# A hybrid decoder layer on one core: the merge of the attention groups' outputs is put behind the sample's third group and the fourth head pair

## The chip, the core and the metric

The kernel runs on one core of a Trainium2 chip. The core has a TensorE (PE) for matrix products, a VectorE (DVE), a ScalarE (ACT) and a GpSimd (POOL) for element-wise work, and queues of DMA transfers that these engines or SyncE (SP) issue. Each engine runs its own instructions in the order in which the program emitted them, and waits for the others at semaphores. The metric is the device time of one execution in microseconds (us).

## The reference, cut to what matters

One inference step of one layer: a prompt of 512 tokens and 8 sample tokens (each with a cache of 4096 positions) pass the same weights. On the same normalised input run an attention in three groups (windows 128, 512 and 2048 with dilations 1, 4 and 16; 8 heads of 64 each) and an RWKV-7 recurrence with 16 heads. The three groups' outputs are merged by their log-sum-exp, each branch is projected and multiplied by a sigmoid gate, and an output projection and a SwiGLU follow.

```python
A_GROUPS = ((128, 1), (512, 4), (2048, 16))
...
    s = jnp.einsum('bgnqhd,bgnkhd->bgnhqk', qb.astype(jnp.float32), kb.astype(jnp.float32)) * HEAD_DIM ** -0.5
    p, lse = masked_softmax(s, valid[:, None])
    o = jnp.einsum('bgnhqk,bgnkhd->bgnqhd', p, vb.astype(jnp.float32))
...
    def step(S, inp):
        r_t, w_t, k_t, v_t, kk_t, a_t = inp
        sa = jnp.einsum('bhij,bhj->bhi', S, -kk_t)
        S = (S * w_t[:, :, None, :] + sa[..., None] * (kk_t * a_t)[:, :, None, :]
             + v_t[..., None] * k_t[:, :, None, :])
        return S, jnp.einsum('bhij,bhj->bhi', S, r_t)
```

## The kernel before

All products are of fp32 values that are split in a high and a low part, so that one k-tile of a projection is three matmuls (`hh,whi`, `hl,whi`, `hh,wlo`) of 128 x 260, 260 being half of the 520 tokens. Weights come as `raw` by DMA; ACT makes `whi` of them and DVE `wlo`. Every instruction goes through one helper, so each row of the profile names its line, 380; rows are told apart by their tiles.

The program is written as many small generators, one for each piece of work: the projections, the attention heads of a group, `sample_group(g)` for the sample tokens of group g, the eight head pairs of the recurrence (in steps `pair`, `chain`, group norm, output `OB`), the sixteen gate jobs (products for the sigmoid gates), the projection of the attention branch (pa), of the recurrent branch (pb), and so on. A planner runs them one step at a time at build time. It keeps a model of each engine's clock, plays the recurrence's jobs first where they are ready, and uses pa and the gate jobs as filler for PE. Waits between generators (`wv.until("merge")`, and `wv.take`/`wv.give` for locks) hold only at build time: they decide the order of emission, and the hardware's waits are the data's own.

What the change touches:

- `sample_group(g)` (line 891 on) scans the cache of group g for the eight sample tokens. For the third group (g = 2) these are eight K tiles and eight V tiles `kt` of 128 x 512, each loaded by a DMA that POOL issues, and for each a product and a reduction on DVE. They use two buffers, `kt`. Line 895 lets the third group wait for "merge", as long as `MERGE_AT` is negative.
- `merge()` (line 1489 on) computes the three groups' factors and stores them as `FD` in DRAM. Behind that, for each of four head pairs and three groups, POOL issues loads of a group's output `oo` (from `OTD`) and of its factors `fb` (from `FD`, broadcast to 64 partitions each, two transfers), into the same two buffers `kt`. DVE multiplies, in twelve operations on `oac` and eight on `oo`, and the sum goes to `OAD`.
- Lines 1518 to 1520, between the store of `FD` and the head pairs, make the merge wait for "sample" 2 and "pair" `MERGE_AT` if `MERGE_AT` is not negative.
- The lock "kt" is held by the merge from its first head pair to its last, and the lock "gq" (one buffer, `oac`, also used by the group norm) for each head pair.
- The split of the merged output for the attention branch's projection, `oa_load` (line 1646), waits for "merge" and for the last head pair.

In the old order the merge begins when the third group's heads are done (`rw_open`, line 1099, spawns it), and the sample's third group stands behind it.

Of the kernel before, what the change touches and what calls it, by code (L numbers as in the profile page):

```python
# [36 lines left out]
SHIFT0 = 4608  # L37
GATE0 = 7968
RESERVE = 0
MERGE_AT = -1  # L40
SAMPLE_AT = -1
PLAIN = 4
EARLY = 4
# [422 lines left out]
def program(tc, I, O):  # L466
# [425 lines left out]
    def sample_group(g):  # L892
        if g:
            yield from wv.until("sample", g - 1)
        if g == 2 and MERGE_AT < 0:
            yield from wv.until("merge")
# [592 lines left out]
    def merge():  # L1489
# [27 lines left out]
        G.dma_start(out=FD[:].rearrange("r h g l -> (r h) g l"), in_=ms[:, :, 0])  # L1517
        if MERGE_AT >= 0:
            yield from wv.until("sample", 2)
            yield from wv.until("pair", MERGE_AT)  # L1520
        yield from wv.take("kt")
# [612 lines left out]
```

## Time and profile before

| | |
|---|---|
| median of 3 runs | 1293.06 us |
| lowest and highest run | 1292.16 and 1295.9 us |
| profiled execution, its own time | 1299.81 us |
| its span on the core | 1298.0 us |
| mean granted TensorE clock | 0.985 of full speed |

The page of the profile gives busy times by engine and by line; answers of the trace give the same by stretches of time, by tile, and in order of time. Times in them are from the start of the span. A row in order of time has the start, the duration, the engine, the operation, the tiles (written <- read), the shapes and, in brackets, how long the engine was idle before it and what released it. Buffer numbers are left out there. The prompt's attention fills the span up to about 360 us; the recurrence runs from there to about 825 us; the output projection and the SwiGLU follow.

### The profile page before, as it was taken

How to read it: one execution, taken by the hardware profiler on the slowest of the kernel's cores; microseconds unless marked ns; L12 is line 12 of the kernel's file. 1: busy time of each engine (PE TensorE's matmuls, PEld its weight loads, DVE VectorE, ACT ScalarE, POOL GpSimd, SP SyncE). 2: the span in 40 equal slices, each digit the busy share in tenths (PEclk: the TensorE clock that was granted, in tenths of full speed). 3: DMA queues.
4: the chain of work that ended last, by engine and by line, in shares of the span. 5: the costliest groups of instructions: out<-in, count | busy, mean ns of one | idle time of the engine just before them, and what ended most of it. 6: DMA issues, size and time to landing. Idle time of an engine off the chain costs nothing.

```text
span 1298.0 us, 29596 instructions
## 1 busy us (share of the span) xinstructions
PE 1246.1 (96%) x11594; PEld 1178.2 (91%) x11594; DVE 933.4 (72%) x2448; ACT 648.2 (50%) x1638; POOL 176.0 (14%) x273
## 2 busy tenths in 40 slices
PE   7999999999989989999999999999999999999996
PEld 6998999989978888888888888999999999999996
DVE  6956866954769998879886765565798888873333
ACT  5244244266666655576775585323444444442220
POOL 1300100100123332122123112121000000010000
PEclk9999999999999999999998999999999999999998
DMA  6532654644245545553346355465233323343331
GB/s 218 157 95 91 209 178 146 208 137 160 73 121 152 145 143 149 153 156 104 89 126 184 101 168 169 139 218 191 92 99 98 98 98 98 98 143 90 90 103 66
DMA packets 93420, 173.76 MB, mean 134 GB/s; under 512 B 42672, under 2 KB 47824, under 8 KB 93280
## 3 DMA queue, kind: packets, MB, share of 16 engines
q1 hardware_dynamic: 60880, 102.46, 25.8%
q0 software_dynamic: 15792, 50.73, 12.9%
q10 hardware_dynamic: 16608, 18.68, 4.3%
q8 instruction: 91, 1.49, 0.5%
q14 instruction: 49, 0.40, 0.1%
HBM read 135.33 MB, written 30.07 MB: 127 GB/s over the span
## 4 chain that ended last, share of the span: by engine, by line
PE 59%; DVE 18%; issue 11%; DMA 6%; ACT 4%; POOL 2%; SPq 0%; ACTq 0%; DVEq 0%; POOLq 0%
PE mm L380 39%; PE ax L380 15%; PE ch L380 5%; DVE wlo L380 3%; DMA fb<-FD 1%; DVE X L380 1%; DVE xt L380 1%; DMA kt<-vcache 1%; DVE qk L380 1%; DVE raw L380 1%; DMA sw<-raw 1%; DVE sw L380 1%; DVE k L380 1%; DVE GH L380 1%; DVE oac L380 1%
## 5 line engine op out<-in xcount | busy, mean ns | idle before, releaser
L380 PE MATMUL mm<-hh,whi 128*128 128x260 f32 x1136 | 340.3, 300 | 0.8 <-ACT gt L380 0.8
L380 PE MATMUL mm<-hh,wlo 128*128 128x260 f32 x1136 | 326.0, 287 | 7.4 <-DVE wlo L380 7.0
L380 PE MATMUL mm<-hl,whi 128*128 128x260 f32 x1136 | 326.0, 287 | 0.0
L380 ACT CAST whi<-raw 128x1024 fp32r<-128x1024 f32 (+2 forms) x213 | 184.2, 866 | 255.8 <-PE mm L380 185.0
L380 DVE TENSOR_TENSOR wlo<-raw,whi 128x1024 fp32r<-128x1024 f32 (+2 forms) x213 | 211.5, 993 | 86.4 <-ACT whi L380 81.7
L380 PEld LDWEIGHTS mm<-hh,whi 128*128 128x128 f32 x1136 | 215.9, 190 | 13.3 <-issue 5.8
L380 PEld LDWEIGHTS mm<-hh,wlo 128*128 128x128 f32 x1136 | 216.0, 190 | 10.0 <-DVE wlo L380 9.2
L380 PEld LDWEIGHTS mm<-hl,whi 128*128 128x128 f32 x1136 | 215.9, 190 | 1.3
L380 PE MATMUL mm<-fh,whi 128*128 128x260 f32 x308 | 87.2, 283 | 0.3 <-DVE g L380 0.3
L380 PE MATMUL mm<-fh,wlo 128*128 128x260 f32 x308 | 87.1, 283 | 0.0
L380 PE MATMUL mm<-fl,whi 128*128 128x260 f32 x308 | 87.1, 283 | 0.0
L380 PE MATMUL mm<-h2l,whi 128*128 128x260 f32 x264 | 74.8, 283 | 0.0
L380 PE MATMUL mm<-h2h,wlo 128*128 128x260 f32 x264 | 74.6, 282 | 0.0
L380 PE MATMUL mm<-h2h,whi 128*128 128x260 f32 x264 | 74.6, 282 | 0.0
L380 PE MATMUL ax<-h2h,wlo 128*128 128x260 f32 x264 | 74.5, 282 | 0.0
L380 PE MATMUL ax<-h2l,whi 128*128 128x260 f32 x264 | 74.5, 282 | 0.0
L380 PE MATMUL ax<-h2h,whi 128*128 128x260 f32 x264 | 74.3, 281 | 0.0
L380 DVE TENSOR_TENSOR xt<-X,LT 128x60 f32<-128x60 f32 (+24 forms) x248 | 59.7, 241 | 3.6
L380 DVE TENSOR_TENSOR X<-X,xt 128x60 f32<-128x60 f32 (+24 forms) x248 | 56.1, 226 | 3.8
L380 PEld LDWEIGHTS mm<-fh,whi 128*128 128x128 f32 x308 | 58.1, 188 | 0.8 <-issue 0.4
L380 PEld LDWEIGHTS mm<-fh,wlo 128*128 128x128 f32 x308 | 57.9, 188 | 0.0
L380 PEld LDWEIGHTS mm<-fl,whi 128*128 128x128 f32 x308 | 57.9, 188 | 0.0
(427 smaller groups left out, 3122.0 us busy)
## 6 DMA issues: line engine op xcount, KB each, us to landing
raw<-w_in SPq DMA_DIRECT2D x77, 512.0 KB, 4.0
raw<-w_gate SPq DMA_DIRECT2D x22, 512.0 KB, 3.8
raw<-w_up SPq DMA_DIRECT2D x22, 512.0 KB, 3.8
raw<-w_down SPq DMA_DIRECT2D x16, 512.0 KB, 3.5
kt<-kcache POOLq DMA_DIRECT2D x24, 256.0 KB, 3.7
kt<-vcache POOLq DMA_DIRECT2D x24, 256.0 KB, 3.6
sw<-raw ACTq DMA_DIRECT2D x64, 65.0 KB, 3.7
GD<-gt ACTq DMA_DIRECT2D x16, 260.0 KB, 3.0
```

Of the source, the lines that this page charges most:

```text
L380: r = f(*a, **k)
```

## The change

One constant is changed.

```diff
 SHIFT0 = 4608
 GATE0 = 7968
 RESERVE = 0
-MERGE_AT = -1
+MERGE_AT = 3
 SAMPLE_AT = -1
 PLAIN = 4
 EARLY = 4
```

It acts at two places of the code:

```python
        if g == 2 and MERGE_AT < 0:
            yield from wv.until("merge")
...
        if MERGE_AT >= 0:
            yield from wv.until("sample", 2)
            yield from wv.until("pair", MERGE_AT)
        yield from wv.take("kt")
```

So the sample's third group no longer waits for the merge, and the head pairs of the merge wait for that group and for the head pair with index 3, the fourth, of the recurrence. As the planner's clocks and the locks see other work, the order changes from the end of the attention to the beginning of the output projection. The numbers of instructions on each engine stay as they were.

In the rows below, tiles carry the numbers that the program gives them. On DVE, before, at the first head pair of the recurrence (`k` and `sg` are its features, `tw` its scan; `oac` and `oo` are the merge's):

```order
L380 TENSOR_TENSOR wlo_4576<-raw_4457,whi_4575 128x1024
L380 COPY bvs<-tmp_4292 128x8
L380 SCALAR_TENSOR_TENSOR k_4518<-pb_4517,mu,k_4518 128x511
L380 SCALAR_TENSOR_TENSOR k_4518<-shift,mu,k_4518 128x8
L380 TENSOR_SCALAR sg_4743<-k_4518,feat 128x8
L380 TENSOR_TENSOR oac_4633<-oo_4374,fb_4376 128x4x128
L380 SCALAR_TENSOR_TENSOR tw_4630<-smask,tw_4630 128x512
L380 TENSOR_TENSOR oo_4641<-oo_4641,fb_4643 128x512
L380 TENSOR_TENSOR oac_4633<-oac_4633,oo_4641 128x4x128
```

And on DVE now, at the end of the attention heads (`PT` are the last heads' probabilities), where the sample's third group begins (`kt` times `sv`, reduced to `sc`):

```order
L380 COPY PT_4065<-ax_4126 128x512
L380 COPY PT_4065<-ax_4138 128x512
L380 TENSOR_TENSOR kt_4145<-kt_4145,sv_4102 128x512
L380 TENSOR_TENSOR kt_4147<-kt_4147,sv_4102 128x512
L380 TENSOR_REDUCE sc_4144<-kt_4145 128x8
L380 TENSOR_REDUCE sc_4144<-kt_4147 128x8
L380 TENSOR_TENSOR wlo_4250<-raw_4047,whi_4249 128x1024
L380 SCALAR_TENSOR_TENSOR k_4203<-pb_4202,mu,k_4203 128x511
L380 SCALAR_TENSOR_TENSOR k_4203<-shift,mu,k_4203 128x8
L380 TENSOR_TENSOR st_4722<-sv_4102 128x64
L380 TENSOR_SCALAR sg_4314<-k_4203,feat 128x8
```

The first row of the merge now stands about 180 rows of DVE further down, and the cache tiles stand where the merge stood and ahead of it.

On POOL, before, around the store of `FD` (`GH`, `AR` and `st` belong to the recurrence):

```order
L380 DMA FD<-ms 96x1x128
L380 TENSOR_TENSOR GH_4411<-GH_4411,DN_4277 64x8x64
L380 DMA fb_4376<-FD 64x4x128 x2
L380 DMA oo_4641<-OTD 128x512
L380 DMA fb_4643<-FD 64x4x128 x2
L380 DMA oo_4921<-OTD 128x512
L380 DMA fb_4923<-FD 64x4x128 x2
L380 TENSOR_TENSOR st_4603<-st_4603,sg_4290 128x512
```

And on POOL now, around the same store:

```order
L380 DMA kt_4433<-kcache 128x512
L380 DMA kt_4521<-kcache 128x512
L380 TENSOR_TENSOR GH_4450<-GH_4450,DN_4301 64x8x64
L380 DMA FD<-ms 96x1x128
L380 TENSOR_TENSOR AR_4318<-AR_4318,PC_4311 128x448
L380 DMA kt_4589<-kcache 128x512
L380 TENSOR_TENSOR GH_4451<-GH_4451,DN_4301 64x8x64
L380 DMA kt_4731<-vcache 128x512
```

The loads of `fb` stood directly behind the store that they read; now the loads of the cache stand there, and the first load of `fb` comes 18 rows after the store.

On PE, before, at the transposes (`ax<-ident,KB`) of the last head pair's group norm: `hh`, `hl` rows are a gate job's, and `OB` rows the recurrent branch's projection.

```order
L380 MATMUL mm_11568<-hh,wlo_11409 128x260
L380 MATMUL mm_11568<-hh,whi_11408 128x260
L380 MATMUL mm_11568<-hl,whi_11408 128x260
L380 MATMUL ax_11591<-ident,KB_9764 128x128 x4
L380 MATMUL mm_11568<-hh,wlo_11409 128x260
L380 MATMUL mm_11626<-OB_11290,whi_11545 128x260 x2
L380 MATMUL mm_11626<-OB_11290,wlo_11546 128x260
L380 MATMUL mm_11626<-OB_11350,whi_11545 128x260 x2
```

And on PE now, at the same transposes (`OB_11607` is the output of head pair 6, `OB_11721` that of head pair 7, the last):

```order
L380 MATMUL mm_11643<-OB_11607,whi_11399 128x260
L380 MATMUL mm_11643<-OB_11607,wlo_11400 128x260
L380 MATMUL ch_11669<-OB_11607,whi_11603 128x260
L380 MATMUL ch_11669<-OB_11607,wlo_11604 128x260
L380 MATMUL ch_11700<-OB_11607,whi_11603 128x260
L380 MATMUL ch_11700<-OB_11607,wlo_11604 128x260
L380 MATMUL ax_11691<-ident,KB_10009 128x128 x4
L380 MATMUL mm_11590<-OB_11721,whi_11399 128x260
L380 MATMUL mm_11643<-OB_11721,whi_11399 128x260
L380 MATMUL ch_11669<-OB_11721,whi_11603 128x260
```

The gate jobs' rows that stood ahead of the transposes are now further up, all sixteen jobs before the last head pair's chain; behind the transposes the rows that read the last pair's output stand first.

## The prediction

> **What bounds the kernel now.** I read the page's totals first, then busy time by stretches, then the waits and the timeline of the stretches that lose TensorE time.
>
> ```profile
> span 1298.0 us, 29596 instructions
> PE 1246.1 (96%) x11594; PEld 1178.2 (91%) x11594; DVE 933.4 (72%) x2448; ACT 648.2 (50%) x1638; POOL 176.0 (14%) x273
> ```
>
> TensorE (PE) is busy for 96% of the span, so a re-ordering that removes no matmul can only win what PE loses in gaps or at a low clock. Where it loses is read from the stretches; the columns are the stretch, its length, then busy time (and instructions) of PE, weight loads, VectorE (DVE), ScalarE (ACT) and GpSimd (POOL), then the granted clock, the DMA share and GB/s.
>
> ```profile
> 320.00:340.00 20.00, 19.98 (x192) 18.52 (x192) 9.79 (x45) 13.49 (x39) 2.23 (x4) 1.00 0.28 96
> 340.00:360.00 20.00, 20.00 (x169) 19.36 (x168) 18.90 (x40) 10.57 (x26) 3.98 (x4) 1.00 0.22 65
> 360.00:400.00 40.00, 32.84 (x291) 30.66 (x290) 29.01 (x72) 22.11 (x55) 13.80 (x18) 0.96 0.48 134
> 400.00:520.00 120.00, 111.30 (x1134) 100.95 (x1133) 110.39 (x366) 74.71 (x188) 34.44 (x50) 0.99 0.53 143
> 520.00:580.00 60.00, 59.29 (x766) 51.88 (x766) 50.16 (x152) 38.61 (x135) 14.15 (x22) 1.00 0.59 165
> 580.00:600.00 20.00, 16.62 (x184) 14.79 (x183) 17.36 (x57) 15.38 (x46) 3.37 (x3) 0.91 0.26 85
> 600.00:680.00 80.00, 78.90 (x862) 70.40 (x860) 69.85 (x270) 59.64 (x194) 16.24 (x22) 1.00 0.36 108
> 680.00:700.00 20.00, 17.28 (x157) 15.56 (x157) 16.27 (x47) 8.82 (x19) 6.09 (x9) 0.83 0.56 163
> 700.00:800.00 100.00, 99.47 (x1311) 85.90 (x1310) 63.02 (x233) 69.96 (x245) 21.29 (x37) 0.98 0.49 149
> 800.00:822.00 22.00, 19.66 (x194) 18.38 (x193) 13.70 (x40) 8.36 (x18) 3.23 (x6) 0.92 0.46 156
> 822.00:840.00 18.00, 17.35 (x140) 16.73 (x140) 8.95 (x13) 6.00 (x11) 2.15 (x4) 1.00 0.45 138
> 802.50:806.00 3.50, 1.72 (x16) 1.45 (x15) 2.19 (x8) 2.63 (x6) 0.54 (x1) 1.00 0.13 46
> 806.00:809.40 3.40, 3.40 (x29) 3.17 (x28) 3.16 (x11) 0.35 (x1) 0.55 (x1) 0.50 0.67 222
> ```
>
> From 360 to 822 us PE stands idle for about 26 us: 7.2 in 360 to 400, 8.7 in 400 to 520, 3.4 in 580 to 600, 2.7 in 680 to 700, 2.3 in 800 to 822, and little elsewhere. In 400 to 520 the reason is plain: DVE is busy for 110.4 of 120 us, so **DVE is the bound there**, with the merge and the sample's cache scan both in that stretch. The last two rows show a second price: a 3.5 us stretch with PE half idle is followed by one of 3.4 us at half clock, which costs 1.7 us more.
>
> **The change part by part.** No instruction is removed or added; PE's matmuls and DVE's work are the same in number. The merge and the sample's third group exchange places, and the planner, which fills PE's time with whatever is ready, then places the sixteen gate jobs and the output projection otherwise. Four terms follow.
>
> (a) *From 340 to about 540 us.* In the old order the merge starts as soon as the last attention heads are done, and its first steps wait for loads that could not start earlier.
>
> ```profile
> DVE oac L380 <- DMA fb<-FD: 7.2, 2, 6.4
> DVE oo L380 <- DMA fb<-FD: 6.1, 3, 4.1
> ```
>
> ```profile
> 361.99 0.23 DVE L380 TENSOR_SCALAR sg<-k,feat 128x8 f32<-128x8 f32 x1
> 368.63 1.10 DVE L380 TENSOR_TENSOR oac<-oo,fb 128x512 f32<-128x512 f32 x1 [6.41 <-DMA fb<-FD]
> 369.65 1.20 DVE L380 TENSOR_TENSOR_SCAN tw<-smask,tw 128x512 f32<-128x512 f32 x1
> 374.91 0.69 DVE L380 TENSOR_TENSOR oo<-oo,fb 128x512 f32<-128x512 f32 x1 [4.05 <-DMA fb<-FD]
> ```
>
> The waits rows read: in total, times, longest. DVE's queue is in order, so the scan at 369.65, which the recurrence needs, stands 6.4 us behind the broadcast factors fb. These waits sum to 7.2 + 6.1 = 13.3 us, and they go, because FD is written long before the merge now reads it. In their place DVE gets the cache tiles, whose loads can stand ahead of it too:
>
> ```profile
> L380 DVE TENSOR_TENSOR kt<-kt,sv x24: 672/688/712, 112.2 to 548.8; 128x512 f32<-128x512 f32 x24
> L380 DVE TENSOR_REDUCE sc<-kt x24: 667/679/705, 113.4 to 550.8; 128x8 f32<-128x512 f32 x24
> ...
>   DMA kt<-kcache: 7.2, 7
>   DMA kt<-vcache: 6.8, 5
> ```
>
> ```profile
> L380 DVE TENSOR_TENSOR oac<-oac,oo x8: 1079/1100/1132, 375.6 to 498.8; 128x512 f32<-128x512 f32 x8
> L380 DVE TENSOR_TENSOR oac<-oo,fb x4: 1074/1107/1125, 368.6 to 478.1; 128x512 f32<-128x512 f32 x4
> ```
>
> All 48 tiles of the three sample groups cost DVE 14.0 us of load waits, sixteen of them a third of that; with what the later merge still waits for its own two buffers I take +4 (0 to +14). Then the work that comes forward. At the first matmul of the third gate job the old order has the whole merge ahead on DVE (12 products of 1.10 us and 8 of 0.69, 18.7 us; the 0.69 is the 374.91 row) and nothing of the sample's third group. The new order has that group's 16 tiles (16 x (0.688 + 0.679) = 21.9 us) and three of four head pairs of the merge (9 x 1.10 + 6 x 0.69 = 14.0 us). So DVE must do 21.9 + 14.0 - 18.7 = +17 us more before that point. DVE was idle for 10.2 us in 320 to 340, where cache tiles can go now; I let that hide 6 of the 17, leaving 11. In sum -13.3 + 4 + 11 = **+2 us** (-8 if 10 more hide in the idle time; +8 if little does).
>
> POOL's queue is in order as well: a cache load that waits for one of the two kt buffers holds back the recurrence's products on POOL behind it. The merge's loads did the same in the same queue, with longer steps (1.10 against 0.69 us), so I cost this at 0, with the bounds of (a) for its own.
>
> (b) *From 580 to 700 us.* What DVE has done earlier it need not do later: the same 17 us. There PE lost 3.4 + 1.1 + 2.7 = 7.2 us, and the clock rows 0.91 and 0.83 another 1.8 + 3.4 = 5.2 us, next to a DVE that was 81 to 87% busy. Not all of it is DVE's: some of these waits are the chain's own latency, below. Of 12.4 I take **-8 us** (-12 to 0).
>
> (c) *The recurrence's last steps.* The gate matmuls are the filler between the dependent steps of the recurrence. In the old order two gate jobs (the fifteenth and sixteenth) still stand beside the last pair; in the new order all sixteen are used up some 600 rows of PE before that pair's end.
>
> ```profile
> PE ch L380 <- ACT GH L380: 2.4, 3, 1.8
> PE ch L380 <- DVE AR L380: 2.2, 2, 1.4
> ```
>
> These are PE's waits on the recurrence from 580 to 822 us with the filler as it was, 4.6 us together. With less of it I take **+3 us** (0 to +5, as if each doubled).
>
> (d) *The end of the last pair.* Here are PE's rows and then DVE's from the last pair's recurrence to its finished output OB.
>
> ```profile
> 811.21 0.67 PE L380 MATMUL ch<-AR 64*64 64x64 f32 x14
> 811.82 0.39 PE L380 MATMUL mm<-hh,whi 128*128 128x260 f32 x1
> 812.04 0.28 PE L380 MATMUL mm<-hl,whi 128*128 128x260 f32 x1
> 812.16 0.28 PE L380 MATMUL mm<-hh,wlo 128*128 128x260 f32 x1
> ...
> 821.83 0.66 PE L380 MATMUL ax<-ident,KB 128*128 128x128 f32 x4 [0.56 <-DVE KB L380]
> ```
>
> ```profile
> 813.52 0.68 DVE L380 TENSOR_REDUCE gm<-ch 128x8 f32<-128x512 f32 x1
> ...
> 817.47 1.22 DVE L380 TENSOR_TENSOR wlo<-raw,whi 128x1024 fp32r<-128x1024 f32 x1
> 818.61 0.16 DVE L380 TENSOR_SCALAR rsy<-gv 128x8 int32<-128x8 int32 x1
> ...
> 821.08 0.69 DVE L380 TENSOR_TENSOR KB<-KB,rsy 128x512 f32<-128x512 f32 x1
> ...
> 826.22 0.69 DVE L380 TENSOR_TENSOR OB<-KB,OB 128x512 fp32r<-128x512 f32 x1 [0.69 <-ACT OB L380]
> ```
>
> The group norm runs on DVE from 813.52 to 821.77; its result is transposed on PE at 821.83, and OB is done at 826.91. Today 77 gate matmuls, 0.12 us apart (812.04 to 812.16), cover the first part up to a wait of 0.56 us, and some 100 others cover the second. In the new order 32 matmuls of the output projection stand between the recurrence and the transposes (twelve of them wait for the head pair before), and the next row after the transposes needs this very OB. The latency from the end of the recurrence (811.88) to OB (826.91) is 15.0 us, less the split wlo that stood in DVE's way, 818.61 - 817.47 = 1.1 us: 13.9. PE has 32 x 0.12 = 3.8 us of matmuls and 0.5 us of transposes for it. It idles for 13.9 - 4.3 = 9.6 us where it idled for 0.56: **+9 us** (+4 if the recurrence itself is over earlier relative to other work; +13 if ACT and DVE have another split or two of weights in front of the norm). Behind such a gap comes low clock, by the pair of rows 802.5 to 809.4: one or two stretches of 3.4 us at 0.50, 1.7 or 3.4 us, where one is seen today: **+1 us** (0 to +3).
>
> The Trainium skill, page "TensorE: Matmul & The Clock Gate", section "Why this matters for your kernels", says that gaps of more than about 3 us between bursts of matmuls are to be avoided, since one idle window brings half rate. That rule speaks against this change, since (d) makes two gaps of 4 to 5 us. Taken alone it would give no low clock today, where PE was idle for 1.8 us, and one such stretch behind each of the two gaps: +3.4 in place of +1, and 1302 us. The rows are harsher, since the half clock came after the 1.8 us all the same; so one of the two stretches is paid today already.
>
> The sum is +2 - 8 + 3 + 9 + 1 = **+7 us**: 1299.8 us, the profiled execution's own time (its span and 1.8 us around it), becomes 1306.8. That execution lies 6.7 us above the median of the three runs, 1293.06, so I carry the difference over: **1300 us**.
>
> **The rivals.** *Faster*: the cover that (d) loses matters less than the waits that go. The mechanism is the one at 368 us: the recurrence's scan stood behind fb, 13.3 us of waits in a stretch in which DVE is the bound. If DVE's idle 10.2 us before 340 us takes the brought-forward work nearly whole, (a) is -8, (b) -12, (c) +2, and (d) with the clock +7: -11, so 1282 us. It decides as soon as (a) and (b) together are under -13. For it speaks that PE's idle time is 16 us in 360 to 520; against it, that DVE at 110 of 120 us leaves no room for anything to come forward. *No change*: the losses and gains cancel, because the matmuls are the same and a gate job that covered the end now fills a hole at 400 to 520 instead: +2 - 10 + 2 + 6 = 0, 1293 us. It needs PE's idle time only to move. *Slower by more*: nothing hides in (a), +8, (b) only -4, the others as in the sum, +13: +17, 1310 us. *The change does nothing*: the order of DVE and PE differs from 320 us on for hundreds of rows, so this is no case.
>
> **How the numbers follow.** About 0.3%, 4 us, is what a measurement of this kernel can tell from no change. The forecast with its worse neighbour (over 1297) gets 0.50, no change 0.25, faster 0.25. The two ends of all terms added up would be 1276 and 1323, which needs every one on the same side; 8 in 10 lie within 1283 to 1312, which reaches to the faster rival at its less favourable end and just past the slower one. The forecast's own range is 1297 to 1310.
>
> **What would show it.** Right: no wait of DVE for fb above 1 us; kt steps in 330 to 440 us; DVE less busy in 580 to 700 and PE's idle time there under 3 us; and two gaps of PE, 4 us or more each, around the last transposes before the output projection, with a clock of 0.50 behind them. Wrong: if PE has other work behind these transposes, (d) falls and the time is under 1293; if the fb waits come back at the merge's new place, or DVE is over 95% busy in 340 to 520 while PE loses 20 us there, the time is above 1310.

## The result, and the profile after

| | before | changed |
|---|---|---|
| median of 4 runs | 1294.48 us | 1317.72 us |
| lowest and highest run | 1292.16 and 1301.29 us | 1314.15 and 1321.49 us |
| profiled execution's span | 1298.0 us | 1318.2 us |
| mean granted clock in it | 0.985 | 0.974 |

The ratio is 1.0156, with a 95% interval from 1.0113 to 1.0199: slower, by about 20 us. The direction was forecast; the time lies above the range (1283 to 1312). In one of the runs below, with the gate jobs kept (1340.39 us), the whole execution was slow at a clock of 0.958, and its ratio leaves that run out.

First the page's totals of the changed kernel, as shown of before.

```profile
span 1318.2 us, 29596 instructions
PE 1261.2 (96%) x11594; PEld 1190.2 (90%) x11594; DVE 934.6 (71%) x2448; ACT 648.4 (49%) x1638; POOL 178.8 (14%) x273
```

The work is the same: DVE, ACT and POOL are busy as long as before. PE is busy 15.1 us longer with the same 11594 instructions, so its matmuls took longer, and idle 5.1 us longer (57.0 against 51.9). The clock agrees: one minus the mean granted clock, times the span, is 34 us against 19. Now the stretches, with the columns of before.

```profile
320.00:340.00 20.00, 19.98 (x189) 18.52 (x187) 11.23 (x35) 14.56 (x45) 1.91 (x6) 1.00 0.38 117
340.00:360.00 20.00, 17.88 (x162) 17.20 (x158) 19.48 (x52) 10.66 (x24) 6.11 (x8) 1.00 0.29 90
360.00:400.00 40.00, 35.17 (x297) 33.22 (x296) 33.96 (x90) 22.98 (x59) 8.46 (x12) 0.87 0.47 130
400.00:520.00 120.00, 110.60 (x1059) 101.78 (x1058) 108.43 (x350) 70.77 (x173) 37.85 (x53) 0.93 0.52 145
520.00:580.00 60.00, 58.47 (x686) 49.16 (x686) 44.84 (x154) 31.93 (x106) 14.63 (x21) 0.91 0.47 127
580.00:600.00 20.00, 20.00 (x259) 18.02 (x259) 14.56 (x59) 15.11 (x58) 0.00 (x0) 1.00 0.29 91
600.00:680.00 80.00, 77.67 (x876) 70.17 (x873) 44.17 (x135) 57.50 (x180) 9.52 (x14) 0.96 0.37 107
680.00:700.00 20.00, 19.66 (x168) 17.44 (x167) 18.61 (x60) 8.99 (x25) 7.09 (x7) 1.00 0.48 138
700.00:800.00 100.00, 96.82 (x1157) 84.75 (x1157) 80.80 (x304) 62.56 (x187) 28.72 (x43) 0.98 0.54 154
800.00:822.00 22.00, 22.00 (x303) 18.98 (x302) 10.63 (x38) 17.23 (x74) 3.88 (x8) 1.00 0.44 147
822.00:840.00 18.00, 16.22 (x187) 13.53 (x186) 9.86 (x30) 10.51 (x39) 3.75 (x7) 1.00 0.45 139
840.00:860.00 20.00, 14.21 (x74) 12.74 (x73) 12.93 (x29) 5.87 (x10) 2.15 (x4) 0.74 0.32 107
```

The last row is the place to look: 74 matmuls in 20 us and a clock of 0.74. The holes of 580 to 600 and 680 to 700 are gone, as forecast, with a DVE that is less busy there (103.5 us of 120 before, 77.3 now). New is the low clock between 360 and 580 us.

Stretches of two kernels with another order can't be subtracted. So I matched them by work: each matmul gets its usual distance to the next (the lower quartile of its kind over all traces); at equal sums of these distances the times are compared. The numbers are how many us a kernel's profiled execution is behind that of before, at the place where before stood at the time in the first row.

```text
before at (us)              400   520   540   580   700   780   809   829   840   870
changed                    +3.0  +6.5 +12.2 +14.0  +8.7  +3.2  +2.7 +10.5 +20.6 +20.6
sample first, merge next   +1.4  +5.0  +4.1  +4.8  +0.3  +1.8  -2.0  -3.7  -3.7  -3.7
lock passed on             +1.9  +2.8  +3.0  +6.4 +11.2 +14.7  +9.3  +9.1  +9.2  +9.1
gates kept                 -5.7  -0.8  +4.8  +6.6  +1.7 +21.6 +21.1 +22.4 +22.4 +22.5
norm held, nothing else    +0.6  +1.9  +1.9  +4.0  +1.2  -3.0  -4.0  +9.6 +17.4 +17.5
norm held half as long     +1.7  +1.9  +2.1  +4.1  -2.7  -8.8  -9.5  -6.7  +1.1  +1.1
merge last                 -0.0  -1.3  +0.9  +1.4  +0.2 +15.7 +13.4 +17.1 +17.1 +17.2
```

Two things limit what this table can tell. Each row is one execution: "gates kept" has the changed kernel's order on every engine to beyond 700 us and is yet 8.7 us away from it at 400 and 7.4 at 580. And a second count by the same method, with kinds told apart by tiles and shapes, agrees within 3 us up to 700 and from 829 on, but is up to 8 us away at 780 and 809.

Of the changed kernel: 14 us are lost by 580, 11 won back by 809, and 17.9 lost from there to 840, at the last head pair's end (16.7 and 23.2 by the second count). Here are its PE rows at that place, in order of time.

```profile
842.76 0.51 PE L380 MATMUL mm<-OB,whi 128*128 128x260 f32 x2 [1.27 <-ACT OB L380]
...
845.36 0.66 PE L380 MATMUL ax<-ident,KB 128*128 128x128 f32 x4 [0.59 <-DVE KB L380]
849.82 0.80 PE L380 MATMUL mm<-OB,whi 128*128 128x260 f32 x2 [3.81 <-ACT OB L380]
850.42 0.64 PE L380 MATMUL ch<-OB,whi 128*128 128x260 f32 x2
850.86 0.42 PE L380 MATMUL mm<-OB,whi 128*128 128x260 f32 x1
851.07 0.42 PE L380 MATMUL mm<-OB,wlo 128*128 128x260 f32 x1
```

The row behind the transposes waits 3.8 us for the last pair's OB, and behind it matmuls start 0.21 us apart in place of 0.12: half clock, for three stretches of 3.4 us.

DVE's waits on loads from 340 to 560 us (in total, times, longest):

```profile
DVE kt L380 <- DMA kt<-vcache: 5.1, 3, 2.1
DVE oac L380 <- DMA fb<-FD: 5.1, 3, 2.6
...
DVE kt L380 <- DMA kt<-kcache: 2.6, 1, 2.6
```

They are 12.8 us where fb alone had 13.3: the waits for fb came back in part at the new place, and the cache tiles have their own.

### The profile page after: what moved, and what is told of

The parts are those of the page before. It is cut to its first block, busy times and chain, and to the rows that moved or that the text cites. A ratio compares the mean times of both kernels' runs of the same rounds, so it can differ in the third digit from the quotient of the medians.

```text
span 1318.2 us, 29596 instructions
## 1 busy us (share of the span) xinstructions
PE 1261.2 (96%) x11594; PEld 1190.2 (90%) x11594; DVE 934.6 (71%) x2448; ACT 648.4 (49%) x1638; POOL 178.8 (14%) x273
## 4 chain that ended last, share of the span: by engine, by line
PE 58%; DVE 16%; issue 12%; DMA 7%; ACT 4%; POOL 2%; SPq 0%; ACTq 0%; DVEq 0%; POOLq 0%
PE mm L380 40%; PE ax L380 14%; PE ch L380 4%; DVE wlo L380 2%; DMA fb<-FD 2%; DMA kt<-vcache 1%; DMA sw<-raw 1%; DVE xt L380 1%; DVE X L380 1%; DVE GH L380 1%; ACT KB L380 1%; DVE oac L380 1%; DVE raw L380 1%; DVE KB L380 1%; DMA xt<-xT 1%
## 5 line engine op out<-in xcount | busy, mean ns | idle before, releaser
L380 DVE TENSOR_TENSOR xt<-X,LT 128x48 f32<-128x48 f32 (+23 forms) x248 | 58.9, 238 | 4.0
L380 DVE TENSOR_TENSOR X<-X,xt 128x48 f32<-128x48 f32 (+23 forms) x248 | 56.2, 227 | 4.1
L380 ACT ACTIVATE GH<-ch,DN 64x64 f32<-64x64 f32 x128 | 39.6, 309 | 39.8 <-PE ch L380 37.4
```

Source lines behind the costliest of these rows:

```text
L380: r = f(*a, **k)
```

## The experiments

What puts the last pair's end late? In the order of emission the fifth head pair starts 389 rows of PE later than before (row 4600 against 4211; here and below this is the row at which its preparation is done, counted in the program). By then five of the sixteen gate jobs and a part of the sixth are emitted, before none (the first begins at row 4224). The pair waits for the first group norm, since it takes over that pair's buffers. The group norm's last part needs the lock "gq" for its tile `bvr`, and the merge holds that same lock: it gives it back after each head pair and takes it again in the same step, so nobody gets between. Before, the merge was over (row 3698) ahead of the first chain's end (3935). Now it runs from the fourth pair to row 4376, and the norm waits. Two rows of the tile `bvr` show it, first and last start in us; before:

```profile
L380 POOL DMA_DIRECT2D bvr<-BVD x8: 536/537/543, 503.1 to 817.8; - x8
L380 DVE SCALAR_TENSOR_TENSOR KB<-KB,feat,bvr x8: 741/750/993, 565.5 to 824.1; 128x512 f32<-128x512 f32 x8
```

and of the changed kernel, in which the merge's last product with `fb` starts at 552.8 us:

```profile
L380 POOL DMA_DIRECT2D bvr<-BVD x8: 536/536/579, 561.7 to 842.3; - x8
L380 DVE SCALAR_TENSOR_TENSOR KB<-KB,feat,bvr x8: 744/752/753, 614.8 to 847.6; 128x512 f32<-128x512 f32 x8
```

The first norm's load comes 59 us later, right behind the merge, and the last pair's norm 23.5 us later. That is theory "lock"; its rival is theory "VectorE", the load brought forward. The experiments ran on four chips, and each ratio is against runs of the kernel before on the same chip; versions on different chips are compared by their ratios.

**Sample first, merge directly behind it.**

```diff
-MERGE_AT = 3
+MERGE_AT = 0
```

> MERGE_AT = 0: the sample's third group still goes first, but the merge follows directly behind it, since the first head pair is done by then. The merge then ends some 280 rows of PE earlier than with 3, the first group norm stands 270 rows earlier, and three gate jobs stand behind the attention branch's projection again. Theory 'lock' (the late merge holds the buffer that the group norm needs, so the fifth head pair starts late, the gate jobs are used up in the meantime, and the last pair's end has no cover): back at the time of the kernel before or better, 1285 to 1297 us. Theory 'VectorE' (the sample's scan and the merge brought forward overload VectorE from 420 to 580 us): still slow, 1305 to 1315 us.

Measured: 1.0015 of before (0.9986 to 1.0045), median 1298.18 us beside 1297.76. No loss, although the scan is as early as in the changed kernel. The last pair's norm:

```profile
L380 DVE SCALAR_TENSOR_TENSOR KB<-KB,feat,bvr x8: 741/748/1139, 583.1 to 814.6; 128x512 f32<-128x512 f32 x8
```

It starts 9.5 us earlier than before. So the sample's group can go first without a loss; "VectorE" has its first miss.

**Merge late, sample behind it as before.**

```diff
-        if g == 2 and MERGE_AT < 0:
+        if g == 2:
...
-            yield from wv.until("sample", 2)
```

> The other part alone: the merge waits for the fourth head pair, and the sample's third group still waits for the merge. The scan is not brought forward; the group norm is as late as in the changed kernel and the gate jobs are used up as early. Theory 'lock': as slow as the changed kernel or a little slower, 1310 to 1325 us, with two gaps at the end of the last pair. Theory 'VectorE': between the two kernels or at before's time, 1290 to 1303 us.

Measured: 1.0271 (1.0224 to 1.0318), median 1330.8 us. The second half alone costs more than the whole change, and more than either theory said. By the second count it is 19 us behind at 580, ahead again at 809 and 28.5 behind at 840: the changed kernel's path, with the scan where it was.

**The lock passed on.**

```diff
             acc = None
+            if hp > 1:
+                yield from wv.until("gn", hp - 2)
             yield from wv.take("gq")
```

> The changed kernel, with one more wait in the merge: its third head pair waits for the first group norm and its fourth for the second, so that the group norm gets the shared buffer in between. The scan stays brought forward as in the changed kernel. Theory 'lock': the fifth head pair starts at 206 rows' distance from before instead of 389 later, the gate jobs last, and the time is before's or better, 1283 to 1297 us. Theory 'VectorE': as slow as the changed kernel, 1308 to 1320 us.

(The expectation's count is garbled: the fifth pair starts at row 4206, against 4211 before and 4600 in the changed kernel.) Measured: 1.0072 (1.0032 to 1.0113), median 1304.41 us. That lies between the two theories, outside the range of each. Over half of the loss is gone, with the scan as early and the merge as late in its start; the table shows nothing lost any more from 809 us on. What stays, 9 us by the table, is lost between 540 and 780 us.

**The gate jobs kept for the end.**

```diff
+HOLD = 4
...
-        if pas and (("oa",) in wv.flags or not fill) and (len(pas) % 2 or not fill or len(fill) <= 2 * len(pas)):
+        if pas and (("oa",) in wv.flags or len(fill) <= HOLD) and (len(pas) % 2 or not fill or len(fill) <= 2 * len(pas)):
```

> The changed kernel, in which the last four gate jobs are not used before the attention branch's projection. The lock stays as late as it is. Theory 'lock', in its last step (the cover of the end): PE's idle time from 800 to 870 us falls from 7.6 to under 2 us and the low clock there with it, while some idle time comes back at 740 to 780 us, where those jobs stood: 1300 to 1310 us. Theory 'VectorE': nothing but the end changes, 1305 to 1312 us, with the loss at 420 to 600 us as it is. If the end's cover doesn't matter: 1315 to 1322 us.

Measured: 1.0176 (1.0134 to 1.0219), median 1321.78 us, which misses both theories' ranges. The end is covered, as the table shows (+21.1 at 809, +22.4 at 870), and nothing is won: the hole moved to 700 to 780 us, where PE now has these rows:

```profile
700.00:740.00 40.00, 35.07 (x417) 30.91 (x415) 34.08 (x127) 26.92 (x87) 12.74 (x16) 0.91 0.47 127
740.00:780.00 40.00, 36.10 (x346) 28.12 (x344) 26.16 (x117) 18.47 (x57) 13.01 (x22) 0.75 0.46 133
```

The miss teaches most. With four gate jobs held back the planner goes on to the attention branch's projection before its input is there, and PE waits for that input (2.9 us for `r` and 1.5 for `ta`, from 730 to 800 us). So the place of the gate jobs alone does not bring the time back. My reading is that the recurrence ends late, and that there is only so much other work to put beside it; where that is put decides where PE waits.

**The norm held back, nothing else changed.** This is the kernel before, with one wait more:

```diff
+        if p == 0:
+            yield from wv.until("sample", 2)
         yield from wv.take("gq")
         bvr = r2.tile([128, T], FP, name=nm("bvr"), tag="gq")
```

> The kernel before, with the merge and the sample's third group where they were; only the first group norm is held back until the sample's third group is done, which puts it at row 4588 of PE (4199 before, 4530 in the changed kernel) and the fifth head pair at 4642 (4211 and 4600). All gate jobs are then used up by row 5507, as in the changed kernel (5515). Theory 'lock': slower than before by 15 to 25 us, 1313 to 1323 us, with two gaps of PE of 4 us or more at the end of the last pair. Theory 'VectorE': at before's time, within 5 us.

Measured: 1.0159 (1.0130 to 1.0188), median 1318.31 us beside 1298.72. The delay of one group norm, with merge and scan where they were, gives a loss as large as the change's. The path to it differs: by the table 4 us are lost by 580, where the changed kernel has lost 14, and 21 from 809 on. So the delay is enough for the loss at the end; the loss by 580 it does not give. Its last norm is as late as the changed kernel's,

```profile
L380 DVE SCALAR_TENSOR_TENSOR KB<-KB,feat,bvr x8: 741/750/754, 591.9 to 846.5; 128x512 f32<-128x512 f32 x8
```

and PE waits for the last OB as there (waits of PE from 800 to 880 us; the changed kernel's row is 5.8, 3, 3.8):

```profile
PE mm L380 <- ACT OB L380: 5.0, 2, 3.8
```

**The scan made lighter.**

```diff
+            V.skip = g == 2
             V.tensor_tensor(out=kt[:], in0=kt[:], in1=_bc(sv[:, 0].unsqueeze(1), [128, KR, 64]), op=ALU.mult)
+            V.skip = False
```

(the same at the product with `sc`; a skipped operation is counted by the planner, but not emitted)

> The changed kernel in the same order, with the sixteen products of the sample's third group left out (the scan's reductions and loads stay), so that VectorE has 16 x 0.69 = 11 us less to do between 340 and 480 us; the sample's output is not the reference's. Theory 'lock': the loss at the end stays, 0 to 8 us faster than the changed kernel. Theory 'VectorE': the loss from 420 to 580 us goes for its most part, 9 to 14 us faster.

Measured: 1.0160 (1.0131 to 1.0189), median 1318.99 us, against 1.0156 of the changed kernel. 11 us less of VectorE's work in its busiest stretch bring no gain that the intervals show; 9 to 14 us would have shown. The changed kernel's row from 400 to 520 us had DVE busy for 108.43 us and PE for 110.60; now it is

```profile
400.00:520.00 120.00, 106.96 (x948) 98.81 (x947) 100.08 (x305) 67.36 (x165) 35.91 (x51) 0.91 0.52 136
```

DVE is less busy, and PE is idle for longer and not for less: DVE's load alone does not bound PE there.

**PE kept busy in the two gaps.**

```diff
+        if quick:
+            wps = bank()
+            for _ in range(18):
+                nc.tensor.matmul(wps[:, :128], lhsT=ident[:], rhs=ident[:], start=True, stop=True)
...
+        if quick:
+            for _ in range(14):
+                nc.tensor.matmul(wps[:, :128], lhsT=ident[:], rhs=ident[:], start=True, stop=True)
```

(`quick` holds for the last head pair alone.)

> The changed kernel with 18 extra matmuls (fp32, 128 x 128, on a bank of their own that nothing reads) just ahead of the last pair's transposes and 14 just behind them, some 3.8 and 3 us of work, so that PE is not idle in the two gaps. If the low clock behind the gaps is a cost of its own, the three low stretches at 840 to 860 us become one or none, and the time falls by 2 to 5 us. If the latency of the group norm is all that counts, the time stays, within 2 us.

Measured: 1.0164 (1.0107 to 1.0221), median 1318.94 us, runs from 1311.07 to 1327.32. In the profiled execution the clock at the end is full:

```profile
840.00:860.00 20.00, 18.85 (x149) 17.83 (x149) 13.84 (x22) 7.67 (x11) 3.73 (x7) 1.00 0.47 159
```

and that execution was the fastest of its four. The median did not move. Whether the low clock at the end has a price of its own is not settled: the runs spread by 16 us, more than the 5 us in question.

**The merge later still.**

```diff
-MERGE_AT = 3
+MERGE_AT = 7
```

> MERGE_AT = 7: the merge comes behind the last head pair's preparation, later than in the changed kernel by some 1800 rows of PE. The first four group norms are through by then, so that the fifth head pair starts at row 4194 (4211 before). Theory 'lock': near before, 1290 to 1308 us, faster than with 3, although the change goes further; what stays is that the attention branch's projection comes late (row 5832 against 5566). Theory 'late merge is what costs': slower than with 3, over 1320 us.

Measured: 1.0137 (1.0102 to 1.0173), median 1315.87 us: a miss of theory "lock" in its narrow form. The fifth pair starts in time, but the table shows 15.5 us lost from 700 to 780 us. PE waits for the recurrence there, 12.0 us from 700 to 800 us where before had 0.3; the longest two rows are

```profile
PE ch L380 <- DVE AR L380: 4.9, 5, 1.9
PE ax L380 <- DVE ysq L380: 3.3, 1, 3.3
```

The merge's products stand in the same stretch, from 700.7 to 796 us, and the attention branch's projection, which waits for the merge, begins at 804.5 us (before at 755.2). The gate jobs last until 799.9 us, so there was some other work. A late merge thus costs at this place without the lock; whether by the missing projection or by its own work on DVE and POOL, no run shows.

**Smaller doses of the delay.** As in the run that held the norm, but held only until the fourth head pair's solve is done:

```diff
         if p == 0:
-            yield from wv.until("sample", 2)
+            yield from wv.until("solved", 3)
```

and, for the middle dose, until its inverse is turned:

```diff
         if p == 0:
-            yield from wv.until("sample", 2)
+            yield from wv.until("at", 3)
```

> A smaller dose of the delay alone: the kernel before, with the first group norm held back only until the fourth head pair's solve is done. The fifth head pair then stands at row 4379 of PE (4211 before, 4642 in the run that held it back most, which took 20 us more). If the loss goes with the delay from the start, 168 of 431 rows give 8 us: 1304 to 1310 us. If the work that fills PE's waits has some to spare, nothing is lost until it runs out: 1295 to 1302 us.

> The middle dose: the first group norm held back until the fourth head pair's inverse is turned, the fifth head pair at row 4485. In proportion 274 of 431 rows give 13 us: 1309 to 1315 us. With some filling work to spare: 1302 to 1309 us, between the smaller dose and the largest.

Measured: 1.0033 (1.0007 to 1.0060), median 1301.49 us, with the fifth pair 168 rows late; 1.0002 (0.9979 to 1.0026), median 1298.54 us, with 274 rows; 1.0159 with 431. The first is within what was expected with work to spare, the second is faster than either branch said. It is not in proportion, and not even in order: the smaller dose costs 0.3%, the middle one nothing. That up to 274 rows there is work to spare fits this, but is not shown by itself. In the table the half dose is 9.5 us ahead at 809 and gives all of it back at the end. Its PE wait there and the last norm are in between:

```profile
PE mm L380 <- ACT OB L380: 3.8, 1, 3.8
```

```profile
L380 DVE SCALAR_TENSOR_TENSOR KB<-KB,feat,bvr x8: 739/748/754, 591.9 to 828.5; 128x512 f32<-128x512 f32 x8
```

The first norm starts at 591.9 us in both; so the largest dose does not lose its 20 us by the first norm's own time. The pairs behind it are later there (the sixth starts at row 4772, here at 4707); that this makes the difference is argued, not tested.

**Sample first and the lock passed on.**

```diff
-MERGE_AT = 3
+MERGE_AT = 0
...
+            if hp in {2: 0, 3: 1}:
+                yield from wv.until("gn", {2: 0, 3: 1}[hp])
```

> MERGE_AT = 0 (the sample's third group first, the merge directly behind it) and the lock passed to the first two group norms between the merge's head pairs. The fifth head pair starts at row 4202 (4288 with MERGE_AT = 0 alone, 4211 before), and four gate jobs last beyond row 5530. If the earliness of the recurrence is what counts, faster than MERGE_AT = 0 alone by up to 5 us and faster than before: 1290 to 1296 us. If the merge's late end (row 4798) costs VectorE as in the run that passed the lock at MERGE_AT = 3, up to 10 us slower than before.

Measured: 1.0054 (1.0025 to 1.0083), median 1303.16 us, slower than before as its second branch said. No version beat the kernel before.

**What is left with the lock passed on.** The edits of "the lock passed on" and "the scan made lighter" together.

> What is left when the lock is passed on (0.7% over before at MERGE_AT = 3). The same kernel in the same order, with the sixteen products of the sample's third group left out, 11 us of VectorE between 340 and 480 us; the sample's output is not the reference's. In the changed kernel itself the same edit brought nothing, since its end was bound by the recurrence. If VectorE's early load is what remains, 4 to 10 us less than with the lock passed on alone: 1291 to 1301 us. If it is the low clock and the merge's place behind the fourth pair, within 3 us of it: 1301 to 1308 us.

Measured: 1.0077 (1.0046 to 1.0108), median 1309.34 us, just above both ranges, against 1.0072 with the full scan. VectorE's early load does not show as the cause, though its share in the stretch did fall (127.60 to 117.89 us of the 140 from 340 to 480 us); a gain of less than about 6 us is not excluded by the two intervals. The three kernels in which the merge is stretched between the norms lose 0.5 to 0.8%; which of their waits does it stays open.

## Why the prediction was wrong

The direction was right, and the largest term stood at the right place, the end of the last pair; the time was 5.7 us above the range. The sum was +7 us, the measured change about +20 (23 between the medians). Point by point, with the table by work:

- **(a), to 540 us: +2 forecast, +12.2 measured in this execution**, +4.8 in "gates kept", which has the same order there. Two things were mis-sized. DVE's waits for loads were to fall by 9.3 us (-13.3 + 4); they fell by 0.5, to 5.1 for fb and 7.7 for the cache tiles. And (a) had no term for the low clock: 0.96 and 0.99 became 0.87 and 0.93 in the two stretches from 360 to 520 us, by one minus the clock about 11 us more, and from 520 to 580 us 1.00 became 0.91, 5 us. PE's idle time from 340 to 520 us did not fall at all: 15.9 us before, 16.4 now. That low clock is not simply a loss: "sample first" has seven half-clock steps of 3.4 us from 340 to 580 us, the changed kernel eleven and the kernel before two, and "sample first" ends no later than before. What causes it stays open.
- **(b), 580 to 700: -8 forecast, -5.3 measured**, and PE's idle time there fell from 7.2 to 2.7 us with a relieved DVE, as the text said. Whether DVE's relief did it no run tests: the gate jobs moved as well.
- **(c), the last steps: +3 forecast; from 700 to 809 us it was -6.0** (-12.9 by the second count). There was filler up to this point: the gate jobs last until 770.7 us and the attention branch's projection until 823.4. The cost of (c) came behind it: from 806 to 839.5 us the recurrence's own matmuls (`ch` and `ax` rows on `AR`, `GH` and `VTr`), which PE shows as busy, lie 9.6 us further apart than usual by the same measure as the table, in the kernel before 1.8 us from 809 to 829.
- **(d) and its clock: +10 forecast, +17.9 measured from 809 to 840**, with most of those 9.6 us in it. The mechanism at the very end was right: the row behind the transposes waits 3.8 us for OB, and three low stretches follow. From 822 to 860 us PE's idle time is 7.6 us and the low clock costs 5.1; in the kernel before it is 1.2 and 0.2 from 809 to 840. Of the two gaps of 4 to 5 us one came, of 3.8 us; ahead of the transposes there are 1.0, 1.3 and 0.6.
- **The step that failed** is the one ahead of the terms: "the planner, which fills PE's time with whatever is ready, then places the sixteen gate jobs and the output projection otherwise". It took the gate jobs' new place as given and costed its effects one by one; no term stands for the lock. The runs showed what was behind it: the merge at its new place keeps the shared lock from the first group norm, so the recurrence's second half starts late. Passing the lock on brings the loss from 1.56% to 0.72%; the delay alone costs 1.59%; keeping the gate jobs for the end does not help (1.76%). Seen so, the terms do not add up singly: what is won early by using filler is given back at the end. What stays open is the 0.5 to 0.8% left with the lock passed on, and the 1.37% of the merge put last, where the lock delays nothing.
- **The rivals.** "Faster" needed (a) and (b) together under -13; they came to +6.9, and the waits for loads that were to go stayed. "Slower by more" (1310 us) came nearest, by luck: its +8 in (a) stood for DVE's work that hides in no idle time, not for the low clock. The sign named for a time above 1310, fb waits at the merge's new place, did show.
- The reading that DVE is the bound from 400 to 520 us did not hold in the changed kernel, as the lighter scan shows. The two ends of all terms add up to 1277 and 1322, not 1276 and 1323; nothing hangs on it.
- The rule weighed from the Trainium skill (page "TensorE: Matmul & The Clock Gate", section "Why this matters for your kernels": no gaps of PE over about 3 us) gave one low stretch behind each of two long gaps, +3.4 us. The trace agrees that low clock follows the one long gap, of 3.8 us, but there are three stretches of it; that three in place of one are also +3.4 us is chance.

## What to carry to other kernels

Before costing a moved step by the engines it loads, list the locks and single buffers it holds and who is next in line for them; a step that gives a lock back and takes it again at once starves the others for its whole length. Where an engine is 96% busy with a fixed amount of work, a delay of the dependent chain can be free as long as independent work is left to put beside it (274 rows of delay cost nothing here, 431 cost 1.6%); so compare the chain's end with the end of the filler, and not only the waits on the way. Moving the filler can move the hole and win nothing.

## What the runs showed of the hardware

The same program spreads by more than the 0.3% that the prediction assumed: 16 runs of the kernel before, on one chip, took 1287.23 to 1303.64 us. The granted clock goes with about half of that: it was between 0.981 and 0.992, and the times less (1 - clock) x span lie between 1276.9 and 1285.1 us. Low clock came in steps of 3.41 us at 0.50, each worth up to 1.7 us, one to three in a row in these two kernels and up to five in "sample first and the lock passed on". Without the one at the very end of the program there are 8 of them before (the first at 274 us) and 18 in the changed kernel, which by count is 17 of the 20 us; but the kernel with the norm held lost the same 20 us with 11 such steps, and was idle 8.6 us longer than before where the changed kernel was 5.1. So neither the low clock nor the idle time alone gives the loss. Kernels with the same order up to 580 us have different counts: from 340 to 580 us the changed kernel has 11 steps, with the gate jobs kept 7.
